# Softmax factors 1/sum: spread over partitions through HBM and multiplied on GpSimd, in place of products with the identity

## The chip, the cores and the metric

One core of a Trainium2 chip runs the whole program in one launch. The metric is the device time of one execution in microseconds (us); lower is better. Engines are named as in the profile: PE (TensorE, matmul), PEld (its weight loads), DVE (VectorE), ACT (ScalarE), POOL (GpSimd) and SP (SyncE, which here only issues DMAs). Each engine works through its own instructions in order.

## The reference, cut to what matters

The program is a stack of transformer-like layers on 512 tokens of width 1024 (and 256 context tokens): two layers with four branches each (two of them attention), then an even layer, an odd layer and feed-forward blocks. The change touches three places, all of the form softmax(scores) times values, where the division by the row sum of the exponentials is done at the end, on the product with the values:

```python
def _attend(q, k, v, sink):
    s = jnp.einsum('bqkgd,bnkd->bkgqn', q, k, ...)
    if sink is not None:
        ...
        p = jax.nn.softmax(jnp.concatenate([s, s_sink], axis=-1), axis=-1)[..., :-1]
    else:
        p = jax.nn.softmax(s, axis=-1)
    return jnp.einsum('bkgqn,bnkd->bqkgd', p.astype(v.dtype), v)
```

The places are the attention of layer 0 (tokens and context), that of layer 1 (tokens only), and the latent attention (MLA) of the odd layer, which runs beside a state-space group (S5) whose recurrence has 63 steps.

## The kernel before, in words

The program is written as generators over tiles; a scheduler then sets the order in which each engine gets its instructions, and pools of buffers with a fixed number of slots decide what an instruction has to wait for. Weights come from HBM over one queue of DMAs, which SP issues in order, through a few buffers that are used in turn.

Attention works on pairs of heads. For one pair, one block of 128 queries (`qi`) and one of its two heads (`j`) there is one item, and items pass through a pipeline of three steps: `scores` (PE matmuls, the row maximum on DVE, the exponential on ACT, which also gives the row sum), `transposes` (PE, with the copy out of PSUM by ACT or DVE into a tile named `pt`, or `hlo` in MLA) and `values` (PE, into one PSUM tile `po` in which head j stands on partitions 64 j to 64 j + 63, queries along the free axis). When the last query block of a pair is done, `normalised` is called with that `po` and the sums, which stand with queries on partitions. It takes the reciprocals (L1137), and PE brings each column of them onto 64 partitions by a product of the broadcast column with the identity (L1141, two per query block). ACT copies the result into SBUF (L1144), and DVE multiplies `po` with it (L1145).

There are 16 such calls: 8 in layer 0 (four of 4 query blocks, output `x`, four of 2, output `xc`), 4 in layer 1 (4 blocks, `y`) and 4 in MLA (4 blocks, output `hlo`). In MLA the result goes at once to a helper, `split`: ACT casts it to a high part `hhi` (L258), and POOL takes the rest `hlo` (L259). Both feed the output projection.

In MLA, `scores` also advances the S5 recurrence by a step or so (L2095 to L2099: five small DVE instructions a step, each step needing the one before it). After MLA, PE needs the finished states and some tables that SP fetches from HBM (`s5T`, `s5ca`).

Of the kernel before, what the change touches and what calls it, by code (L numbers as in the profile page):

```python
# [9 lines left out]
F32 = mybir.dt.float32  # L10
# [4 lines left out]
ALU = mybir.AluOpType  # L15
AX = mybir.AxisListType
PSUM = bass.MemoryType.PSUM
P = 128
# [78 lines left out]
class Kern:  # L97
# [254 lines left out]
    def silu_c(self):  # L352

        cc = self.vc[:, 0:16]
        t = self.tl(self.sm, [P, 16], F32, "siluc")
        self.S.activation(t, cc, AF.Tanh, scale=0.5)
        self.V.scalar_tensor_tensor(t, t, 1.0, cc, ALU.add, ALU.mult)
        self.sT = self.tl(self.cp, [P, 8, 32], F32, "sT")
        self.V.memset(self.sT, 0.0)
        for i in range(2):  # L360
            self.V.tensor_scalar(self.sT[:, :, i], t[:, 8 * i:8 * i + 8], 0.5, None, ALU.mult)
# [67 lines left out]
    def layer0_norm(self, i, hcp):  # L429

        xt, nt = self.toks[i]
        ss = self.tl(self.sm, [P, nt], F32, "l0ss")
        sq = self.tl(self.hp, [P, 1024], BF16, "hhi")
        for t in range(nt):
            self.S.activation(sq, xt[:, t, :], AF.Square, accum_out=ss[:, t:t + 1])
        r = self.rsq(ss, 1.0 / 1024, EPS, [P, nt], "nrm")
        for t in range(nt):
            self.V.tensor_scalar(xt[:, t, :], xt[:, t, :], r[:, t:t + 1], None, ALU.mult)
        n = nt * P
        xn = [self.tl(*((self.xp, [P, 512], F32, "x"), (hcp, [P, 256], F32, "xc"))[i]) for _ in range(8)]  # L440
        yield xn, n
        for k in range(8):
            ps = self.tl(self.tp, [P, 512], F32, "tp")
            for t in range(nt):
                self.T.transpose(ps[:, t * P:(t + 1) * P], xt[:, t, k * P:(k + 1) * P], self.ident)
            (self.S.copy if k % 2 else self.V.tensor_copy)(xn[k], ps[:, :n])
            if k == 3:
                yield
        yield
# [683 lines left out]

    def normalised(self, out, po, sums, nq, pool, tag, bufs=None):

        r = self.tl(self.sm, [P, 4, 2], F32, "rsm", bufs=2)
        self.V.reciprocal(r[:, :nq], sums[:, :nq])  # L1137
        pb = self.tl(self.tp, [P, 512], F32, "tp")
        for qi in range(nq):
            for j in range(2):  # L1140
                self.T.matmul(pb[64 * j:64 * j + 64, qi * P:(qi + 1) * P], r[:, qi, j:j + 1].to_broadcast([P, 64]),  # L1141
                              self.ident, start=True, stop=True)
        rb = self.tl(pool, [P, 512], F32, tag, bufs=bufs)
        self.S.copy(rb[:, :nq * P], pb[:, :nq * P])  # L1144
        self.V.tensor_tensor(out, po[:, :nq * P], rb[:, :nq * P], ALU.mult)  # L1145

    def run(self, gen):

# [689 lines left out]
class Kern3(Kern2):  # L1838
# [21 lines left out]

    def s5_alloc(self):
        dp = self.ctx.enter_context(self.tc.tile_pool(name="s5d", bufs=1, space=bass.MemoryType.DRAM))
        self.d_bm = [self.tl(dp, [P, 4, 2, P], F32, f"dbm{b}") for b in range(4)]
        self.d_ca = [self.tl(dp, [P, 2, 8, 64], F32, f"dca{b}") for b in range(4)]
        self.d_kk = self.tl(dp, [16, 32, 15 * 16], F32, "dkk")
        self.d_tt = [self.tl(dp, [P, 4, 4, P], F32, f"dtt{b}") for b in range(2)]
        self.a8 = self.tl(self.cp, [P, 2, 2, 16], F32, "a8")
# [500 lines left out]
```

## Time and profile before

| | |
|---|---|
| time, median of 3 runs | 2815.12 us (2809.93, 2815.12, 2815.5) |
| the profiled execution | 2810.49 us, of which the span is 2808.7 us |
| mean granted clock of TensorE | 0.991 |
| PE busy, share of the span | 2716.6 us, 97% |
| DVE busy | 1423.4 us, 51% |
| ACT busy | 1000.8 us, 36% |
| POOL busy | 895.9 us, 32% |

The span runs from the first to the last instruction; 1.8 us of the profiled execution lie outside it. Busy times are sums over the whole program, whose parts have different limits, and the ends of matmuls are modelled, so that a PE that shows as busy may still be waiting in part. What a change is worth in one part is read from that part.

### The profile page before, as it was taken

What the parts mean: (1) busy time and instruction counts of PE and PEld (TensorE: products, weight loads), DVE (VectorE), ACT (ScalarE), POOL (GpSimd) and SP (SyncE); (2) the same over time, 40 slices, a digit from 0 to 9 for tenths busy, and PEclk for the clock granted to TensorE, in tenths of its full rate; (3) what the DMA queues carried; (4) which work ended last, traced back from release to release, by engine and by line L of the source; (5) the groups of instructions that cost most, each with busy time, mean ns of one, the idle gap of its engine ahead of it and who ended that gap; (6) DMA issues with size and microseconds to landing.
All of it is one profiled execution on the core that took longest, in us unless ns stands there. A gap on an engine that the chain in (4) does not pass through costs nothing. (4 is left out here: it accounts for less than half of the span.)

```text
span 2808.7 us, 39749 instructions
## 1 busy us (share of the span) xinstructions
PE 2716.6 (97%) x15896; PEld 2269.8 (81%) x15896; DVE 1423.4 (51%) x2837; ACT 1000.8 (36%) x1802; POOL 895.9 (32%) x685
## 2 busy tenths in 40 slices
PE   6999999999998999999999989999999989999998
PEld 4976888888897888888998777788888876788888
DVE  5635511113255556435678787655542377655532
ACT  3335522222343553333445332322222244422322
POOL 4500343332234134333322232533333221333332
PEclk9999999999999999999999999999999999999999
DMA  7226122112222114342322231223223212332222
GB/s 247 68 87 201 61 64 75 58 59 66 93 75 90 46 50 121 119 133 75 95 84 75 50 98 35 71 91 105 91 98 97 80 54 83 99 104 90 96 96 87
DMA packets 221581, 250.33 MB, mean 89 GB/s; under 512 B 14351, under 2 KB 205428, under 8 KB 220116
## 3 DMA queue, kind: packets, MB, share of 16 engines
q1 hardware_dynamic: 219204, 242.86, 27.7%
q0 software_dynamic: 2192, 4.93, 0.9%
q8 instruction: 125, 2.05, 0.3%
q14 instruction: 60, 0.49, 0.1%
HBM read 233.64 MB, written 8.88 MB: 86 GB/s over the span
## 5 line engine op out<-in xcount | busy, mean ns | idle before, releaser
L234 POOL TENSOR_TENSOR wlo<-wraw,whi 128x1024 fp32r<-128x1024 f32 (+3 forms) x180 | 438.7, 2437 | 859.0 <-ACT whi L233 826.0
L233 ACT CAST whi<-wraw 128x1024 fp32r<-128x1024 f32 (+2 forms) x360 | 351.9, 1007 | 594.5 <-issue 201.0
L234 DVE TENSOR_TENSOR wlo<-wraw,whi 128x1024 fp32r<-128x1024 f32 (+2 forms) x180 | 235.9, 1310 | 376.9 <-ACT whi L233 376.4
L240 PE MATMUL ex<-hhi,wlo 128*128 128x512 f32 x1044 | 408.2, 391 | 7.1 <-DVE wlo L234 7.1
L238 PE MATMUL ex<-hhi,whi 128*128 128x512 f32 x1044 | 410.1, 393 | 0.6 <-ACT whi L233 0.6
L239 PE MATMUL ex<-hlo,whi 128*128 128x512 f32 x1044 | 408.0, 391 | 0.0
L238 PE MATMUL mm<-hhi,whi 128*128 128x512 f32 x708 | 281.7, 398 | 2.4 <-ACT whi L233 2.2
L239 PE MATMUL mm<-hlo,whi 128*128 128x512 f32 x708 | 278.7, 394 | 3.0 <-DVE hlo L330 2.6
L240 PE MATMUL mm<-hhi,wlo 128*128 128x512 f32 x708 | 278.9, 394 | 2.6 <-DVE wlo L234 2.5
L240 PEld LDWEIGHTS ex<-hhi,wlo 128*128 128x128 f32 x1044 | 196.6, 188 | 49.9 <-DVE wlo L234 8.6
L238 PEld LDWEIGHTS ex<-hhi,whi 128*128 128x128 f32 x1044 | 196.9, 189 | 41.9 <-ACT whi L233 1.6
L239 PEld LDWEIGHTS ex<-hlo,whi 128*128 128x128 f32 x1044 | 196.9, 189 | 39.5 <-issue 0.2
L238 PEld LDWEIGHTS mm<-hhi,whi 128*128 128x128 f32 x708 | 133.9, 189 | 32.5 <-issue 3.6
L240 PEld LDWEIGHTS mm<-hhi,wlo 128*128 128x128 f32 x708 | 133.6, 189 | 32.4 <-DVE wlo L234 3.8
L239 PEld LDWEIGHTS mm<-hlo,whi 128*128 128x128 f32 x708 | 133.9, 189 | 30.9 <-DVE hlo L330 3.9
L238 PE MATMUL mm<-whi,hhi 128*128 128x256 f32 (+1 forms) x464 | 135.2, 292 | 0.5 <-ACT hhi L258 0.5
L240 PE MATMUL mm<-whi,hlo 128*128 128x256 f32 (+1 forms) x464 | 133.2, 288 | 1.4 <-DVE hlo L330 1.4
L239 PE MATMUL mm<-wlo,hhi 128*128 128x256 f32 (+1 forms) x464 | 133.2, 287 | 0.9 <-DVE wlo L234 0.9
L238 PE MATMUL ex<-fhi,whi 128*128 128x512 f32 (+1 forms) x308 | 112.1, 364 | 0.0
L240 PE MATMUL ex<-fhi,wlo 128*128 128x512 f32 (+1 forms) x308 | 111.7, 363 | 0.0
L239 PE MATMUL ex<-flo,whi 128*128 128x512 f32 (+1 forms) x308 | 111.7, 363 | 0.0
L234 POOL TENSOR_TENSOR wblo<-wbraw,wbhi 128x256 fp32r<-128x256 f32 x32 | 27.0, 845 | 238.6 <-ACT wbhi L233 224.4
(823 smaller groups left out, 6019.6 us busy)
## 6 DMA issues: line engine op xcount, KB each, us to landing
wraw<-in_w_merge SPq DMA_DIRECT2D x32, 1024.0 KB
wraw<-in_ev_w_in SPq DMA_DIRECT2D x22, 1024.0 KB
wraw<-in_ffn_gate SPq DMA_DIRECT2D x22, 1024.0 KB
wraw<-in_ffn_up SPq DMA_DIRECT2D x22, 1024.0 KB
wraw<-in_w_in SPq DMA_DIRECT2D x20, 1024.0 KB
wraw<-in_ffn_down SPq DMA_DIRECT2D x17, 1024.0 KB
wraw<-in_w_ada SPq DMA_DIRECT2D x16, 1024.0 KB
wbraw<-in_w_br SPq DMA_DIRECT2D x32, 256.0 KB
```

Source lines behind the costliest of these rows:

```text
L233: self.S.copy(hi[:, a:b], raw[:, a:b])
L234: e.tensor_tensor(lo[:, a:b], raw[:, a:b], hi[:, a:b].bitcast(F32), ALU.subtract)
L238: self.T.matmul(ps, lh, rh, start=first, stop=False)
L239: self.T.matmul(ps, lh, rl, start=False, stop=False)
L240: self.T.matmul(ps, ll, rh, start=False, stop=last)
```

## The change

The reciprocals are written in the order of heads (8 columns, or 4). One PE transpose turns them into 8 rows of 128 (L1141 of the new file), DVE copies them to SBUF (`rrow`, one buffer), SP stores them to HBM (`drr`), and two further DMAs load them back, each spread over 64 partitions, into the tile `rb` that the product with the identity filled before. ACT copies `po` into `out`, and POOL multiplies `out` with `rb` in place. Two small tiles lose their second buffer.

```diff
     def normalised(self, out, po, sums, nq, pool, tag, bufs=None):
 
-        r = self.tl(self.sm, [P, 4, 2], F32, "rsm", bufs=2)
-        self.V.reciprocal(r[:, :nq], sums[:, :nq])
-        pb = self.tl(self.tp, [P, 512], F32, "tp")
-        for qi in range(nq):
-            for j in range(2):
-                self.T.matmul(pb[64 * j:64 * j + 64, qi * P:(qi + 1) * P], r[:, qi, j:j + 1].to_broadcast([P, 64]),
-                              self.ident, start=True, stop=True)
+
+        n = nq * P
+        r = self.tl(self.sm, [P, 8], F32, "rsm", bufs=1)
+        self.V.reciprocal(r[:, :2 * nq].rearrange("p (j q) -> p q j", j=2), sums[:, :nq])
+        pr = self.tl(self.tp, [P, 512], F32, "tp")
+        self.T.transpose(pr[:2 * nq, :P], r[:, :2 * nq], self.ident)
+        rows = self.tl(self.cp, [8, P], F32, "rrow")
+        self.V.tensor_copy(rows[:2 * nq], pr[:2 * nq, :P])
+        d = self.tl(self.drp, [8, P], F32, "drr")
+        self.nc.sync.dma_start(d[:2 * nq], rows[:2 * nq])
+        self.S.copy(out, po[:, :n])
         rb = self.tl(pool, [P, 512], F32, tag, bufs=bufs)
-        self.S.copy(rb[:, :nq * P], pb[:, :nq * P])
-        self.V.tensor_tensor(out, po[:, :nq * P], rb[:, :nq * P], ALU.mult)
+        for j in range(2):
+            self.nc.sync.dma_start(rb[64 * j:64 * j + 64, :n], d[j * nq:(j + 1) * nq].rearrange("q t -> (q t)").unsqueeze(0)
+                                   .to_broadcast([64, n]))
+        self.G.tensor_tensor(out, out, rb[:, :n], ALU.mult)
...
     def s5_alloc(self):
         dp = self.ctx.enter_context(self.tc.tile_pool(name="s5d", bufs=1, space=bass.MemoryType.DRAM))
+        self.drp = self.ctx.enter_context(self.tc.tile_pool(name="drr", bufs=4, space=bass.MemoryType.DRAM))
```

The scheduler lays the instructions out anew, and three places of the order matter below. Line numbers up to L1133 are the same in both files, and later ones are higher by 6 or 7 in the new one (the exponential of MLA is L2209 before and L2216 now, the row maximum L1297 and L1303).

ACT's order at the end of MLA's first pair, before: the copy of the spread factors (L1144), the cast of the normalised tile (L258), and behind it the exponentials of the next pair (L2209), each with what it waits for.

```order
L2209 ACTIVATE hhi_20628,sme_20569<-mat_20623,mx_20626 128x256 [waits DVE_49,Activation_49]
L1144 COPY hlo_20661<-tp_20652 128x512 [waits PE_49,Activation_49]
L258 CAST hhi_20647<-hlo_20649 128x512 [waits DVE_49]
L2209 ACTIVATE hhi_20671,sme_20569<-mat_20666,mx_20669 128x256 [waits DVE_49,Activation_49]
L2222 COPY hlo_20680<-tp_20678 128x128 [waits PE_49]
L2209 ACTIVATE hhi_20702,sme_20569<-mat_20697,mx_20700 128x384 [waits DVE_49,Activation_49]
```

The same place now: `hlo_20655` is the unscaled copy of `po`, and the cast of it waits for POOL, that is, for the multiplication.

```order
L2216 ACTIVATE hhi_20634,sme_20575<-mat_20629,mx_20632 128x256 [waits DVE_49,Activation_49]
L1146 COPY hlo_20655<-mpo_20509 128x512 [waits PE_49,Activation_49]
L2171 COPY mkT_20694<-tp_20696 64x512 [waits PE_49,Pool_49]
L258 CAST hhi_20653<-hlo_20655 128x512 [waits Pool_49]
L2216 ACTIVATE hhi_20676,sme_20575<-mat_20671,mx_20674 128x256 [waits DVE_49,Activation_49]
L2229 COPY hlo_20685<-tp_20683 128x128
L2216 ACTIVATE hhi_20707,sme_20575<-mat_20702,mx_20705 128x384 [waits DVE_49,Activation_49]
```

The cast keeps its place ahead of the next pair's exponentials, but what it waits for is now POOL instead of DVE. It is so at the end of the second and third pair too.

DVE's order at the end of MLA's last pair, before: from the copy of the last transposed block (L2222) over the last reciprocal to the first addition of the residual (L1283); between the reciprocal and the multiplication L1145 stand 25 instructions of the recurrence, and 17 behind that.

```order
L2222 COPY hlo_21166<-tp_21161 128x512
...
L1137 RECIPROCAL rsm_21192<-sme_20991 128x8
L2095 TENSOR_TENSOR s5ta_19926<-a_21_117,xp_3306_19848 128x32
...
L1145 TENSOR_TENSOR hlo_21191<-mpo_21106,hlo_21203 128x512
L2095 TENSOR_TENSOR s5ta_19926<-a_21_117,xp_3306_19848 128x32
...
L1283 TENSOR_TENSOR x_6687<-mm_21225,x_6687 128x512
```

The same place now, with the two copies of transposed blocks ahead of it.

```order
L2105 TENSOR_TENSOR xp_3330_19854<-s5ta_19932,s5tb_19933 128x32
L2106 TENSOR_TENSOR xp_3330_19854<-s5ta_19932,s5tb_19933 128x16
L2229 COPY hlo_21107<-tp_21104 128x256
L1303 TENSOR_REDUCE mx_21132<-mat_21129 128x1
L2229 COPY hlo_21145<-tp_21141 128x384
L1303 TENSOR_REDUCE mx_21154<-mat_21151 128x1
L2229 COPY hlo_21169<-tp_21164 128x512
L1139 RECIPROCAL rsm_21195<-sme_20995 128x4x2
L1143 COPY rrow_21199<-tp_21197 8x128
L1289 TENSOR_TENSOR x_6697<-mm_21227,x_6697 128x512
```

No step of the recurrence is left behind the last reciprocal: the 42 instructions that stood there (8.4 steps) have moved ahead. In the first interval between two reciprocals stand 17.0 steps now where 9.6 stood, in the second 14.4 (9.4), in the third 4.6 (8.4). In the first interval 10 steps stand together between two maxima, and only one copy (L2229) breaks them.

SP's order at the end of MLA, before: `s5T` and `s5ca` are the S5 tables (1 MB and 0.5 MB each).

```order
L226 DMA wraw_21517<-in_od_w_out 128x4x256 [waits DMAHW5_49,DVE_49,Pool_49]
L2256 DMA s5T_3603_21278<-dtt_19_115 128x2048 [waits PE_49,DVE_49,Activation_49,Pool_49]
L2261 DMA s5ca_3606_21282<-dca_14_110 128x1024
L2261 DMA s5ca_3607_21283<-dca_16_112 128x1024 [waits DMASW3_49,DMAHW2_49,DMASW2_49,DMASW0_49]
L2263 DMA s5T_3604_21279<-dtt_20_116 128x2048 [waits DMAHW3_49]
```

The same place now, from the last pair's store on.

```order
L1145 DMA drr_21201<-rrow_21199 8x128 [waits DMAHW5_49,DVE_49]
L2263 DMA s5T_3635_21280<-dtt_19_117 128x2048 [waits PE_49,DMAHW6_49,Activation_49,Pool_49]
L1149 DMA hlo_21204<-drr_21201 64x512 [waits DMAHW4_49,DMAHW5_49,DMAHW3_49,Pool_49]
L1149 DMA hlo_21204<-drr_21201 64x512 [waits DMAHW0_49]
L2268 DMA s5ca_3638_21284<-dca_14_112 128x1024 [waits DMAHW1_49]
L2268 DMA s5ca_3639_21285<-dca_16_114 128x1024 [waits DMASW3_49,DMASW2_49,DMASW0_49]
L2270 DMA s5T_3636_21281<-dtt_20_118 128x2048
```

The last pair's store stands first, the first S5 table between the store and the two loads of the factors, and the other tables behind them.

## Rows read from the trace of the kernel before

**Rows 1.** The page, part 1: busy time, share of the span, instructions.

```profile
PE 2716.6 (97%) x15896; PEld 2269.8 (81%) x15896; DVE 1423.4 (51%) x2837; ACT 1000.8 (36%) x1802; POOL 895.9 (32%) x685
```

**Rows 2.** Windows: length; busy us (instructions) of PE, PEld, DVE, ACT, POOL; clock, DMA.

```profile
206.00:275.00 69.00, 69.00 (x612) 45.74 (x610) 36.09 (x85) 37.52 (x89) 0.00 (x0) 1.00 0.61 196
275.00:315.00 40.00, 37.89 (x361) 30.42 (x360) 23.44 (x71) 27.12 (x69) 4.97 (x3) 1.00 0.33 105
940.00:1015.00 75.00, 74.41 (x683) 61.31 (x681) 40.59 (x84) 46.65 (x99) 10.83 (x7) 1.00 0.18 47
2297.00:2342.00 45.00, 44.84 (x353) 31.19 (x351) 43.32 (x199) 26.30 (x74) 6.51 (x7) 0.98 0.04 13
```

**Rows 3.** Line L1141: ns min/median/max, first and last start.

```profile
L1141 PE MATMUL tp<-cst,rsm x224: 272/273/323, 218.9 to 2351.8; 128*64 128x128 f32 x112
```

**Rows 4.** Timeline, two calls in layer 0 (start, us, engine, line).

```profile
218.87 1.04 PE L1141 MATMUL tp<-cst,rsm 128*64 128x128 f32 x16
219.85 0.39 PE L1076 MATMUL at<-tk,tq 128*128 128x256 f32 x1
...
228.62 0.66 PE L1141 MATMUL tp<-cst,rsm 128*64 128x128 f32 x8
```

**Rows 5.** Timeline, one PE transpose in MLA and what follows it.

```profile
2312.77 0.28 PE L2220 MATMUL tp<-cst,hhi 128*128 128x128 f32 x1
...
2312.89 0.81 PE L2203 MATMUL mat<-mkT,mqT 96*128 96x384 f32 x2
```

**Rows 6.** Waits of 206 to 320 us: total, times, longest.

```profile
PE at L1076 <- ACT e L1089: 1.7, 3, 0.7
```

**Rows 7.** Timeline, end of MLA's first pair.

```profile
2310.39 0.29 DVE L2222 COPY hlo<-tp 128x128 f32<-128x128 f32 x1
...
2311.11 1.14 PE L1141 MATMUL tp<-cst,rsm 128*64 128x128 f32 x15
...
2311.42 0.22 DVE L2095 TENSOR_TENSOR s5ta<-a,xp 128x32 f32<-128x32 f32 x1
...
2312.24 0.21 DVE L2095 TENSOR_TENSOR s5ta<-a,xp 128x32 f32<-128x32 f32 x1
...
2312.96 0.69 DVE L1145 TENSOR_TENSOR hlo<-mpo,hlo 128x512 f32<-128x512 f32 x1
...
2313.68 0.62 ACT L258 CAST hhi<-hlo 128x512 fp32r<-128x512 f32 x1 [0.76 <-DVE hlo L1145]
...
2314.32 0.47 ACT L2209 ACTIVATE hhi<-mat,mx 128x256 f32<-128x256 f32 x1
...
2314.45 1.27 POOL L259 TENSOR_TENSOR hlo<-hlo,hhi 128x512 fp32r<-128x512 f32 x1 [8.22 <-ACT hhi L258]
```

**Rows 8.** Timeline of SP's DMA issues (us of issuing), a store and load through HBM.

```profile
1238.53 4.82 SPq L1986 DMA_DIRECT2D dkk<-s5kk  x6
...
1245.35 2.07 SPq L1996 DMA_DIRECT2D dtt<-dkk  x3
```

**Rows 9.** DMA issues: count, KB each, median us to landing.

```profile
wf<-in_w_fnet POOLq DMA_DIRECT2D x2, 64.0 KB, 2.4
bsp<-in_b_sp POOLq DMA_DIRECT2D x4, 64.0 KB, 4.1
```

**Rows 10.** Timeline, end of MLA's last pair and start of S5.

```profile
2348.68 0.20 DVE L1137 RECIPROCAL rsm<-sme 128x8 f32<-128x8 f32 x1
...
2351.08 0.32 PE L1141 MATMUL tp<-cst,rsm 128*64 128x128 f32 x1
...
2354.38 1.30 DVE L2096 TENSOR_TENSOR s5tb<-a,xp 128x32 f32<-128x32 f32 x1
...
2355.67 0.50 PE L239 MATMUL mm<-hlo,whi 128*128 128x512 f32 x1 [0.39 <-POOL hlo L259]
...
2358.20 0.18 DVE L2099 TENSOR_TENSOR xp<-s5ta,s5tb 128x16 f32<-128x16 f32 x1
...
2360.79 0.67 PE L2273 MATMUL ex<-s5ca,xp 64*64 64x128 f32 x16
```

More of the change, by code (lines that the diff above doesn't have):

```diff
@@ L354, in silu_c @@
         cc = self.vc[:, 0:16]
-        t = self.tl(self.sm, [P, 16], F32, "siluc")
+        t = self.tl(self.sm, [P, 16], F32, "siluc", bufs=1)
         self.S.activation(t, cc, AF.Tanh, scale=0.5)
@@ L431, in layer0_norm @@
         xt, nt = self.toks[i]
-        ss = self.tl(self.sm, [P, nt], F32, "l0ss")
+        ss = self.tl(self.sm, [P, nt], F32, "l0ss", bufs=1)
         sq = self.tl(self.hp, [P, 1024], BF16, "hhi")
```

## The prediction, made before the changed kernel ran

> **What bounds the kernel now.** I began with the busy times of the page [rows 1]: PE is the only engine near its limit over the whole program, so an instruction taken from PE is worth something wherever PE really sets the pace. The windows by stage [rows 2] say where that is. In the attention of layer 0 (206 to 275 us) and layer 1 (940 to 1015) PE is busy for 69.00 of 69 and 74.41 of 75 us, and DVE and ACT are half idle. From 275 to 315 PE has 37.89 of 40, so a little is already waited for there. MLA (2297 to 2342) is another case: PE shows 44.84 of 45, but its ends are modelled, its weight loads fill only 31.19, and DVE is busy for 43.32 of 45, or 96%. DVE carries both the row maxima of the attention and the recurrence, and there I take it, with PE's chain, for the bound.
>
> **What is removed from PE.** The trace has 224 of the old products [rows 3]. They are pipelined, so their price is not 273 ns each: a group of 16 holds PE for 219.85 - 218.87 = 0.98 us [rows 4], a group of 8 for half, 0.49 (its busy time, 0.66, is the upper bound). One transpose takes their place. Transposes of 128x128 follow each other or another matmul after 0.12 us and show 0.28 busy [rows 5]; I take 0.12. Layer 0 saves 4 x 0.86 + 4 x 0.37 = 4.9 us, layer 1 saves 4 x 0.86 = 3.4, together **-8.3 us** where PE is the bound. With 0.28 it would be -6.4, and with 0.66 for a group of 8, -9.0. MLA's four calls are counted in its chain below.
>
> **What the new path costs in layers 0 and 1 (12 calls).** The result isn't wanted before the merge, much later, and ACT's copy of `po` waits only for PE. So the round trip through HBM is hidden by the items that follow, as long as there are buffers. Three things are not hidden for certain. `rb` holds one of the four `pt` slots until POOL has multiplied, some 7 us instead of 2; the order has copies into `pt` that now wait for POOL. POOL's multiplication can hold up DVE (next paragraph but one), and the maximum of an item with a sink is a DVE instruction of two SBUF operands ahead of an exponential. And the scheduler has put scores and exponentials in another order. Before, the waits of PE for exponentials were 1.7 us in three, 0.7 the longest [rows 6]. I take a wait of about half of 0.7 for each of the 12 calls, **+4 us**; the lower end is 0, the upper 12 x 0.7 = +8.
>
> **What it costs in MLA.** Here the cast of the normalised tile stands in ACT's order ahead of the exponentials of the next pair, and keeps that place (first piece of the order). Before, from the first of 15 products at 2311.11 to the next exponential at 2314.32 there were 3.2 us [rows 7]. Now the chain is: transpose 0.28 [rows 5]; copy to `rrow` 0.29, as the nearest DVE copy of 128 columns [rows 7]; issue of the store 0.7 and of the two loads 1.4 (issues on SP took 4.82/6 = 0.8 and 2.07/3 = 0.69 each [rows 8]); the store's landing; the loads' landing; the multiplication on POOL, 1.27 by the 512-column row, and the cast 0.62 [rows 7]. For the store, the last one to `dkk` was issued by 1243.35 and the load of it at 1245.35, so 2.0 us at most [rows 8]; for the loads, a 64 KB transfer showed 2.4 [rows 9]. Both are of another size or queue; the ends I keep are 1 and 4.1 us each (half the first row, and the slower 64 KB row of [rows 9]). With 2.0 and 2.4 the sum is 9.0 us, with the ends 6.6 and 12.8. ACT thus comes free for the next pair 5.8 us later than before, at three boundaries.
>
> [...]
>
> What hides this is the recurrence. A step takes 2312.24 - 2311.42 = 0.82 us of DVE [rows 7]. The order moves 8.4 steps from behind the last reciprocal to ahead of it, most of them into the first two boundaries, where DVE is then busy while ACT waits. But DVE was full already, so this only shifts the last reciprocal: +8.4 x 0.82 = +6.9, less 3 x (0.69 - 0.29) = 1.2 for the multiplications that leave DVE [rows 7]. In the third boundary only 1.6 steps and three maxima (about 2.6 us as an estimate, a maximum being put at half a step) are left between the copy to `rrow` and the copy that needs the exponentials. Of the chain 9.0 - 0.6 = 8.4 us come after `rrow`, so DVE and PE stand idle for about 5.8. At the end of the last pair there were 9.7 us from the products (2351.08) to the first use of `s5ca` (2360.79) [rows 10], PE filling them with the output projection. Now the chain to the cast takes 9.0, the issue of a 1 MB table stands between store and loads (0.7), POOL makes the low part after the cast (1.27), and a last matmul follows: about 11.5, so +1.8. Nothing of the recurrence hides that any more.
>
> One thing more speaks against the change. At 2354.38 a step's small DVE instruction took 1.30 us where one takes 0.21 [rows 7, 10]. It ran beside POOL's part of the last split, for which the matmul at 2355.67 then waits, so I read it as 1.1 us in which POOL held DVE. The four new multiplications are as long. In three of them DVE is in the recurrence; I take one hit in all, +1.0, the ends being 0 and 3.3.
>
> [...]
>
> MLA's sum is 6.9 - 1.2 + 5.8 + 1.8 + 1.0 = +14.3 us. Some will come back: the stretches without recurrence steps have a lighter DVE, and PE takes matmuls of the output projection into the boundaries, so that fewer are left at the end. I take **+12 us**, with ends of +4 (the short landings, and the idle time of the third boundary filled) and +21 (the long landings, three hits).
>
> **The sum** is -8.3 + 4 + 12 = about +7.7 us. Against the profiled execution (2808.7 of span and 1.8 around it, 2810.49) that is 2818. The profiled execution lies 4.6 us under the median of the runs, 2815.12, so I put the forecast at **2822 us**, +0.25%. Both ends together give -9.0 + 0 + 4 = -5 and -6.4 + 8 + 21 = +23, so 2810 and 2838.
>
> **Rivals.** (a) *Hidden in MLA, faster.* The total work of DVE in MLA falls (by 4 x 0.40 = 1.6 us), and if DVE alone sets the pace there, waits of ACT that DVE fills with steps of the recurrence cost nothing. The total would be -8.3 + 2 - 1.6 = about -8, 2807. For it speaks DVE's 96%; against it that the steps run out before the third boundary, and that nothing of DVE's work is left for the last chain. It decides if the chain after `rrow` is shorter than about 5 us, which wants landings near 1 us. (b) *Even.* MLA costs only 5 to 8 us, and the two sides cancel within 0.2% of the time (5.6 us, about what a measurement of this kernel can tell from no change). The rows for it are those of (a), with one boundary idle. (c) *The chain shows in the layers too.* If `rb` in a `pt` slot stops the transposes at each of the 12 calls for about 2 us (a chain of 9.0 against three items of the pipeline, some 7 us), 12 x 2 instead of 4 makes it +28, 2843. For it speak the new waits for POOL in the order, against it that ACT and DVE have half their time free there [rows 2].
>
> **How the numbers follow.** My forecast, slower by 6 to 23 us, has a chance of 0.52; (a) 0.15, (b) 0.24, (c) 0.09. So faster by over 0.2% 0.15, within it 0.24, slower 0.61. The range of 8 in 10 reaches from 2808 (most of (b), the upper part of (a)) to 2840.
>
> **What would show it.** Right: the L1141 group falls from 224 matmuls to 16 transposes; ACT's cast (L258) in MLA waits 4 us or more for POOL each time; PE has idle stretches of 3 us or more at the third boundary and at the end of MLA; the stretch of layer 1's attention becomes shorter by 2 us or more. Wrong: MLA's stretch from its first reciprocal to the first `s5ca` matmul doesn't grow by 4 us (then (a) holds), or the store and loads land in about 1 us each; or PE in layer 0 and 1 waits more than it saves (then (c)). The step I trust least is what the recurrence hides in MLA.

## The result, and the profile after

The changed kernel takes 2848.71 us (median of 4 runs, 2845.07 to 2851.14) against 2815.31 for the kernel before on the same chip (4 runs): a ratio of 1.0131, with a 95% interval of 1.0119 to 1.0143. It is slower by some 33 us where about 7 were forecast, and lies outside the 2810 to 2838 us of the forecast. Its profiled execution took 2847.89 us, with a span of 2846.0 and a mean granted clock of 0.985 (0.991 before).

Page of the changed kernel, part 1, which answers to [rows 1]:

```profile
PE 2727.9 (96%) x15688; PEld 2262.6 (79%) x15688; DVE 1426.5 (50%) x2837; ACT 999.0 (35%) x1802; POOL 915.5 (32%) x701
```

The 208 records taken from PE are gone (224 for 112 products before, 16 for 16 transposes now), and yet it shows 11 us more of busy time: what is left runs slower somewhere. Line L1141, with the store and POOL's multiplication in MLA (ns min/median/max, first and last start), answers to [rows 3]:

```profile
L1141 PE MATMUL tp<-cst,rsm x16: 271/273/273, 218.7 to 2378.7; 128*8 128x128 f32 x12, 128*4 128x128 f32 x4
L1145 SPq DMA_DIRECT2D drr<-rrow x16: 246/296/354, 219.3 to 2379.3; - x16
L1151 POOL TENSOR_TENSOR hlo<-hlo,hlo x4: 1261/1262/1311, 2324.7 to 2387.4; 128x512 f32<-128x512 f32 x4
```

Before, the first of the products began at 218.9 [rows 3] and the last call's first one at 2349.6 (shown below); now the two stand at 218.7 and 2378.7. So 29 of the 37.3 us by which the span grew are lost between them, and the other 8 behind. Windows of the changed kernel (columns as in [rows 2]):

```profile
206.00:275.00 69.00, 66.67 (x529) 41.46 (x527) 32.74 (x80) 33.99 (x82) 3.26 (x3) 1.00 0.64 205
2297.00:2342.00 45.00, 35.05 (x218) 23.07 (x219) 43.16 (x211) 20.71 (x59) 6.30 (x7) 0.85 0.10 31
2342.00:2395.00 53.00, 39.88 (x225) 24.66 (x225) 26.33 (x107) 15.32 (x42) 8.90 (x7) 0.84 0.21 75
```

In layer 0 PE now has 2.3 idle us of 69, where it had none. In MLA it is busy for 35.05 of 45 instead of 44.84, and the granted clock there is 0.85, where it was 0.98: PE waits, and in between it runs in part at half clock (a granted clock of 0.50 from 2326.7 to 2333.5). Not all of that drop is new: 6.8 us at half clock ahead of the first call (2299 to 2306) are a stretch that the kernel before has too, at 2292 to 2299, most of it outside the window.

To place the loss I matched the instructions of DVE, ACT and POOL that both kernels have (same line, same tile, same place in the count) and took the median shift of their starts in quiet stretches ahead of, between and behind the three attention stages. Differences of neighbouring shifts say by how much a stage grew: layer 0 +7.90 us, layer 1 -1.04, MLA with the following S5 products **+28.40**; the stretches between them +0.21 and +0.95. The same for every experiment, with its time:

| kernel | median us | ratio to before (95%) | layer 0 | layer 1 | MLA |
|---|---|---|---|---|---|
| changed | 2848.71 | 1.0131 (1.0119 to 1.0143) | +7.90 | -1.04 | +28.40 |
| e1_layers_new | 2819.46 | 1.0030 (1.0021 to 1.0039) | +8.08 | -1.09 | -0.64 |
| e2_mla_new | 2842.59 | 1.0106 (1.0089 to 1.0123) | +0.03 | -0.05 | +28.08 |
| e7_old_finish | 2847.75 | 1.0133 (1.0118 to 1.0148) | +8.20 | +0.17 | +27.52 |
| e6_old_spread | 2826.82 | 1.0064 (1.0046 to 1.0081) | +2.79 | +0.88 | +8.93 |
| e3_cast_pool | 2846.04 | 1.0124 (1.0109 to 1.0140) | +8.12 | -1.08 | +30.89 |
| e10_cast_pool_late_proj | 2848.62 | 1.0130 (1.0111 to 1.0150) | +7.96 | -1.08 | +31.03 |
| e9a_rec_first_new | 2849.22 | 1.0128 (1.0099 to 1.0158) | +9.61 | -1.02 | +29.13 |
| e9b_rec_first_old | 2815.51 | 1.0012 (1.0001 to 1.0022) | +0.01 | +0.01 | +1.77 |
| e11a_short_rec_new | 2844.94 | 1.0126 (1.0109 to 1.0143) | +7.96 | -1.07 | +23.19 |
| e11b_short_rec_old | 2811.36 | 1.0000 (0.9991 to 1.0009) | 0.00 | -0.10 | +0.36 |
| e13_three_freed | 2828.80 | 1.0061 (1.0048 to 1.0074) | +6.52 | -1.08 | +11.87 |
| e4_fill | 2852.73 | 1.0144 (1.0129 to 1.0159) | +9.76 | -1.05 | +30.72 |
| e4b_fill15 | 2841.29 | 1.0097 (1.0077 to 1.0118) | +7.63 | -1.07 | +18.35 |
| e17a_cast_only | 2852.52 | one run | +7.88 | -1.07 | +27.58 |
| e17b_cast_only_fill | 2837.13 | one run | +7.67 | -1.09 | +17.86 |
| e14a_slot_new | 2833.77 | 1.0082 (1.0067 to 1.0097) | -5.08 | -2.06 | +23.40 |
| e14b_slot_old | 2811.59 | 0.9997 (0.9988 to 1.0006) | -0.01 | +0.03 | +0.23 |
| e15_slot_layers_only | 2806.13 | 0.9984 (0.9975 to 0.9993) | -5.09 | -2.12 | -0.78 |

In the stretches between the stages, where the kernels have the same code, these shifts still change by up to 4 us, and between layer 1 and MLA by more than 6 in three profiles (e3, e10, e17a). In MLA the changed kernel, e2 and e14a have the same order on every engine and lost 28.4, 28.1 and 23.4. So a difference of 2 us in a layer, or of 5 in MLA, decides nothing by itself.

**MLA after.** The timeline from the end of the first pair, which answers to [rows 7] (start, us, engine, line; in brackets the idle time and what ended it):

```profile
2318.87 0.27 PE L1141 MATMUL tp<-cst,rsm 128*8 128x128 f32 x1
2319.18 0.28 DVE L1143 COPY rrow<-tp 8x128 f32<-8x128 f32 x1 [0.24 <-PE tp L1141]
2319.49 0.30 SPq L1145 DMA_DIRECT2D drr<-rrow  x1
2321.08 1.12 SPq L1149 DMA_DIRECT2D hlo<-drr  x2
...
2324.68 1.31 POOL L1151 TENSOR_TENSOR hlo<-hlo,hlo 128x512 f32<-128x512 f32 x1 [10.92 <-DMA hlo<-drr]
...
2324.89 1.16 DVE L2105 TENSOR_TENSOR xp<-s5ta,s5tb 128x32 f32<-128x32 f32 x1
...
2326.02 0.62 ACT L258 CAST hhi<-hlo 128x512 fp32r<-128x512 f32 x1 [3.54 <-POOL hlo L1151]
2326.69 0.80 PE L238 MATMUL mm<-hhi,whi 128*128 128x512 f32 x1 [3.72 <-ACT hhi L258]
...
2334.12 0.69 ACT L2216 ACTIVATE hhi<-mat,mx 128x512 f32<-128x512 f32 x1 [4.99 <-DVE mx L1303]
...
2340.88 0.27 PE L1141 MATMUL tp<-cst,rsm 128*8 128x128 f32 x1
...
2361.44 0.27 PE L1141 MATMUL tp<-cst,rsm 128*8 128x128 f32 x1
...
2378.67 0.27 PE L1141 MATMUL tp<-cst,rsm 128*8 128x128 f32 x1
```

The chain that was forecast is there, link by link: transpose 2318.87, copy 2319.18, store 2319.49, loads 2321.08, POOL 2324.68, cast from 2326.02 to 2326.64. That is 7.8 us, a little shorter than the forecast 9.0. What is not there is its price. From one call to the next lie 22.0, 20.6 and 17.2 us. Before, the first product of each of the four calls stood so:

```profile
2311.00 0.27 PE L1141 MATMUL tp<-cst,rsm 128*64 128x128 f32 x1
...
2325.28 1.04 PE L1141 MATMUL tp<-cst,rsm 128*64 128x128 f32 x16
...
2338.94 0.27 PE L1141 MATMUL tp<-cst,rsm 128*64 128x128 f32 x1
...
2349.64 0.32 PE L1141 MATMUL tp<-cst,rsm 128*64 128x128 f32 x1
```

That is 14.3, 13.7 and 10.7 us apart. So the three boundaries lost 7.7, 6.9 and 6.5 us, together 21.2. The rest, 7.6, is behind the last call: from there to the last matmul of `s5ca` it took 25.3 us and takes 32.8.

Three waits tell who stood in line. ACT waits 3.54 for POOL. PE waits 3.72 for ACT: a matmul of the output projection (L238), which needs that very tile, has been put into the boundary. And the first exponential of 512 columns waits 4.99 for a maximum of DVE and begins 7.5 us after the cast was done. The waits of 2316 to 2392 us (total, times, longest):

```profile
ACT hhi L258 <- POOL hlo L1151: 20.6, 4, 7.6
...
PE mm L238 <- ACT hhi L258: 12.6, 4, 4.0
```

And the windows of 6 us across the first boundary:

```profile
2318.00:2324.00 6.00, 4.96 (x37) 3.15 (x35) 5.58 (x29) 1.58 (x4) 0.00 (x0) 1.00 0.16 48
2324.00:2330.00 6.00, 3.31 (x7) 1.55 (x8) 5.69 (x25) 2.75 (x9) 2.58 (x2) 0.72 0.00 2
2330.00:2336.00 6.00, 5.30 (x28) 3.09 (x28) 5.72 (x28) 1.15 (x3) 1.23 (x2) 0.71 0.00 0
```

The reader is to see three things at once: DVE full, PE with 7 instructions in 6 us where [rows 7] has 15 in 1.14, and the clock at 0.72 and 0.71, mixed from stretches at 1.00 and 0.50. Each could be the reason.

### The profile page after: what moved, and what is told of

Its sections match the earlier page's. It is cut to its first block, busy times and chain, and to the rows that moved or that the text cites. A ratio compares the mean times of both kernels' runs of the same rounds, so it can differ in the third digit from the quotient of the medians.

```text
span 2846.0 us, 39499 instructions
## 1 busy us (share of the span) xinstructions
PE 2727.9 (96%) x15688; PEld 2262.6 (79%) x15688; DVE 1426.5 (50%) x2837; ACT 999.0 (35%) x1802; POOL 915.5 (32%) x701
## 4 chain that ended last, share of the span: by engine, by line
PE 43%; DVE 6%; DMA 2%; issue 1%; ACT 1%; POOL 1%; SPq 0%; ACTq 0%; POOLq 0%; DVEq 0%
PE ex L238 7%; PE ex L239 7%; PE ex L240 7%; PE mm L238 5%; PE mm L239 5%; PE mm L240 5%; DVE xs L1536 1%; PE sg L1700 1%; DVE wlo L234 0%; ACT whi L233 0%; PE mpo L2240 0%; DMA dcol<-in_ev_d_skip 0%; DMA dk<-dk 0%; PE mat L2210 0%; DMA hlo<-drr 0%
## 5 line engine op out<-in xcount | busy, mean ns | idle before, releaser
L234 POOL TENSOR_TENSOR wlo<-wraw,whi 128x1024 fp32r<-128x1024 f32 (+3 forms) x180 | 439.2, 2440 | 765.7 <-ACT whi L233 743.9
L234 DVE TENSOR_TENSOR wlo<-wraw,whi 128x1024 fp32r<-128x1024 f32 (+2 forms) x180 | 233.2, 1295 | 375.1 <-ACT whi L233 374.4
L238 PE MATMUL ex<-hhi,whi 128*128 128x512 f32 x1044 | 410.7, 393 | 0.6 <-ACT whi L233 0.5
L238 PE MATMUL mm<-hhi,whi 128*128 128x512 f32 x708 | 283.1, 400 | 15.0 <-ACT hhi L258 12.6
L238 PEld LDWEIGHTS ex<-hhi,whi 128*128 128x128 f32 x1044 | 196.8, 189 | 42.0 <-ACT whi L233 0.9
L238 PEld LDWEIGHTS mm<-hhi,whi 128*128 128x128 f32 x708 | 134.1, 190 | 45.7 <-ACT hhi L258 13.9
L238 PE MATMUL mm<-whi,hhi 128*128 128x256 f32 (+1 forms) x464 | 134.9, 291 | 2.6 <-ACT hhi L258 2.6
L238 PE MATMUL ex<-fhi,whi 128*128 128x512 f32 (+1 forms) x308 | 112.3, 365 | 0.0
L234 POOL TENSOR_TENSOR wblo<-wbraw,wbhi 128x256 fp32r<-128x256 f32 x32 | 26.8, 838 | 205.3 <-ACT wbhi L233 188.6
```

The lines of the kernel that those rows point to most:

```text
L234: e.tensor_tensor(lo[:, a:b], raw[:, a:b], hi[:, a:b].bitcast(F32), ALU.subtract)
L238: self.T.matmul(ps, lh, rh, start=first, stop=False)
```

## The experiments

### Which stage, and which half of the change

e1 gives MLA the old function and leaves the layers new; e2 the reverse.

```diff
-                self.normalised(on, po, st["s", m], 4, self.hp, "hlo")
+                self.normalised_p(on, po, st["s", m], 4, self.hp, "hlo")
```

> The new path in layers 0 and 1 (12 calls), the old products in MLA's four calls. By the shifts between the two traces (about +8 us gained over layer 0, -1 over layer 1, +29 over MLA), the theory that the three places add up expects +7 us against before, 2822, and MLA's stretch as before. A rival, that MLA's loss comes from something that the layers leave behind (loads that arrive later, a shifted queue), expects MLA's stretch long here too, and +20 us or more.

> The old products in layers 0 and 1, the new path in MLA alone. The theory that the places add up expects +29 us against before, 2844. The rival of e1 expects MLA's stretch near that of before, and less than +10 us.

Each stage keeps its own loss to within 0.7 us: +8.08 in layer 0 and -0.64 in MLA for e1, 0.03 and +28.08 for e2. So MLA isn't late because of anything the layers leave behind, and the two can be studied apart.

e7 spreads through HBM, but lets DVE multiply `po` as before; e6 keeps the products with the identity, and copies and multiplies in the new way.

```diff
# e7
-        self.S.copy(out, po[:, :n])
...
-        self.G.tensor_tensor(out, out, rb[:, :n], ALU.mult)
+        self.V.tensor_tensor(out, po[:, :n], rb[:, :n], ALU.mult)
# e6, behind the old products
+        self.S.copy(rb[:, :nq * P], pb[:, :nq * P])
+        self.S.copy(out, po[:, :nq * P])
+        self.G.tensor_tensor(out, out, rb[:, :nq * P], ALU.mult)
```

> The other half: the factors go through HBM, and DVE multiplies po with them as before, so that POOL has no part and DVE, in order, waits for the loads. If the round trip is what costs, layer 0 is slower by 6 us or more and MLA by 20 or more, at least as slow as the changed kernel. If the finish on POOL costs, layer 0 comes out at or under before.

> Half of the change: the factors are spread by the old products on PE, but the result is copied out by ACT and multiplied on POOL. No transfer through HBM. If the round trip is what costs, layer 0 gains or loses less than 2 us and MLA less than 8. If the finish on POOL costs (its hold on DVE, 1.27 more in the chain of MLA), layer 0 is slower by 4 or more and MLA by 10 or more.

The way through HBM alone costs as much as the whole change (+27.5 in MLA, +8.2 in layer 0). The new finish alone costs +8.9 in MLA and +2.8 in layer 0, which lies between the two expectations for e6 and decides for neither. The two halves add up to more than the whole (36.4 and 11.0 against 28.4 and 7.9). In MLA both hold up the same cast, which may be why; no run separates it.

### Is it ACT's queue, PE's, or DVE's?

e3 takes the cast from ACT, so that ACT can go on to the next pair's exponentials.

```diff
-                self.split(hi, lo, on, eng=G)
+                G.tensor_copy(hi, on)
+                G.tensor_tensor(lo, on, hi.bitcast(F32), ALU.subtract)
```

> The changed kernel, but the cast to the high part in MLA is done by POOL behind its multiplication, so that ACT's exponentials no longer stand behind the round trip. Theory A (ACT in order behind the cast is what stops the pairs) expects the three boundaries to fall back to their length of before within 2 us each, some 15 to 20 us of the 29 given back, 2828 to 2833 in all, with the loss at the end of MLA left. Theory B (DVE, full of recurrence steps that were moved, and held by GpSimd's multiplications, sets the pace) expects less than 8 us back, above 2840.

MLA stays at +30.9, so that nothing came back, as theory B had it. But PE also stands still in the boundary, for the tile and not for DVE; the timeline of e3:

```profile
2331.84 0.50 PE L238 MATMUL mm<-hhi,whi 128*128 128x512 f32 x1 [3.88 <-POOL hhi L2246]
...
2333.62 0.37 ACT L2229 COPY hlo<-tp 128x256 f32<-128x256 f32 x1 [4.41 <-PE tp L2227]
```

e10 adds that the projection's sums begin with the third pair's tile, so that none of its matmuls can be put into the first boundaries.

```diff
-        side = self.residual(yd, I["od_w_out_2"][0], 4)
+        side = self.residual(yd, I["od_w_out_2"][0], 4, ks=(2, 0, 1, 3))
```

> The changed kernel with the cast on POOL (as in the earlier run) and the output projection's sums begun with the third pair's tile, so that none of its matmuls can stand in the first two boundaries. Neither ACT nor PE then waits for the round trip there; DVE's order still has the bunched steps (17.4 and 12.6 in the first two intervals). Theory D expects the first interval between the transposes of two pairs, 22 us in the changed kernel, to fall to 17 or less, and the second from 20.5 to 17 or less. Theory B expects 20 to 22 and 18 to 20.

Again nothing: +31.0, with first intervals of 22.9 and 21.4 us, no shorter than theory B expected. The timeline of e10 shows the third queue:

```profile
2334.10 0.42 DVE L2234 COPY hlo<-tp 128x256 f32<-128x256 f32 x1
...
2334.57 0.90 PE L2232 MATMUL tp<-cst,hhi 128*128 128x128 f32 x3 [5.98 <-DVE hlo L2234]
...
2338.04 0.69 ACT L2221 ACTIVATE hhi<-mat,mx 128x512 f32<-128x512 f32 x1 [9.09 <-DVE mx L1308]
```

PE waits 5.98 us for a copy that stands on DVE behind a bunch of recurrence steps: what hid ACT's wait in the forecast is now the wait.

e9a and e9b try to take the bunch away by running the recurrence ahead (`advance(63)` at its definition), in the changed kernel and in the kernel before.

> The changed kernel with all 63 steps of the S5 recurrence emitted ahead of MLA's attention (the result is the same), so that DVE carries only the maxima and copies there. To be read against the next run, the kernel before with the same edit, in MLA's stretch from the first reciprocal to the last use of the S5 tables. Theory B (DVE full of moved steps sets the pace of the boundaries) expects the difference to fall from 29 us to 15 or less. If the round trip itself (ACT behind the cast, PE behind the projection) sets the pace, it stays at 22 or more.

> The kernel before with all 63 steps of the recurrence emitted ahead of MLA's attention: the control of the run before it. Both should lose the cover that the attention gave the recurrence, 63 x 0.82 = 52 us less what the projections hide, so 20 to 45 us slower than before.

This pair is inconclusive. Neither kernel became slower by the 20 us or more that were expected, because the scheduler moved only 5 steps: 32 instead of 27 stand ahead of the first reciprocal, so the bunches stayed (+29.1 and +1.8).

e11a and e11b cut the recurrence to 24 of its 63 steps, again in both kernels; 39 steps are left out of the computation.

```diff
-        V.memset(xp3[:, :, :, 0:1], 0.0)
+        V.memset(xp3, 0.0)
...
-            for c in range(63):
+            for c in range(24):
```

> The changed kernel with the S5 recurrence cut to its first 24 steps (39 steps are left out, their states stay zero, so the output isn't the reference's), all of which stand ahead of MLA's first reciprocal. From there on DVE has only maxima and copies. To be read against the next run, the kernel before with the same cut, from the first reciprocal to the last use of the S5 tables. Theory B (the moved steps on a full DVE set the pace) expects the 29 us between the two kernels to shrink to 12 or less. Theory E (the round trip itself leaves PE without work, whoever stands behind it, and the half clock stretches it) expects 20 or more to stay.

> The kernel before with the same cut (39 of 63 steps left out): the control. If DVE was what set the pace of MLA before, its stretch from the first reciprocal becomes shorter by 8 us or more; if PE did, by less than 4.

This is the plainest answer on the prediction's step about DVE. The kernel before doesn't gain from 39 steps less (ratio 1.0000, MLA +0.4): its calls stand within 1.4 us of where they stood, 14.4 and 14.1 us apart against 14.3 and 13.7, as the timeline of e11b shows.

```profile
2311.82 1.04 PE L1141 MATMUL tp<-cst,rsm 128*64 128x128 f32 x16
...
2326.22 1.04 PE L1141 MATMUL tp<-cst,rsm 128*64 128x128 f32 x16
...
2340.31 0.27 PE L1141 MATMUL tp<-cst,rsm 128*64 128x128 f32 x1
```

So the 96% that DVE shows there are no bound: the steps fill time that is left. And of the changed kernel's loss at most 28.4 - 23.2 = 5.2 us go with the steps, a difference that the clock alone can make (below). Theory E expected 20 or more to stay, and 23 did.

e13 joins e3, e10 and e11a: cast on POOL, projection late, 39 steps left out.

> The changed kernel with all three queues freed at MLA's boundaries: the cast on POOL, the output projection begun with the third pair's tile, and the recurrence cut to its first 24 steps (39 left out, so the output isn't the reference's). To be read against the kernel before with the same cut, whose transposes of the pairs stand 14.4 and 14.1 us apart. If the three in-order queues (ACT behind the cast, PE behind the projection, DVE behind the bunched steps) each hold the boundary alone, the first two intervals fall to 16 or less here, where freeing ACT alone, ACT and PE, or DVE alone left them at 19 to 23. If something else holds them (slots, the round trip itself), they stay at 18 or more.

The transposes of the four calls in e13's timeline:

```profile
2317.58 0.27 PE L1141 MATMUL tp<-cst,rsm 128*8 128x128 f32 x1
...
2331.30 0.27 PE L1141 MATMUL tp<-cst,rsm 128*8 128x128 f32 x1
...
2344.84 0.27 PE L1141 MATMUL tp<-cst,rsm 128*8 128x128 f32 x1
...
2361.50 0.27 PE L1141 MATMUL tp<-cst,rsm 128*8 128x128 f32 x1
```

Two intervals are 13.7 and 13.5 us, below the 14.4 and 14.1 of the control e11b. The round trip is as long as ever (5.9 and 5.5 us from transpose to POOL, 5.8 and 5.5 in the changed kernel) and costs nothing there, once none of the three queues has something of the next pair behind something that waits for it. Freeing one queue (e3, e11a) or two (e10) gave 5 us at most. In the third interval the projection is back in place, and PE alone holds the boundary:

```profile
2352.32 0.79 PE L238 MATMUL mm<-hhi,whi 128*128 128x512 f32 x1 [4.85 <-POOL hhi L2251]
```

The interval is 16.7 us, where the control has 10.7. With the end that leaves +11.9.

### The clock

e4b and e4 put 15 and 30 matmuls (the identity with itself, never read) into each of the three boundaries, ahead of the waiting ones, so that PE doesn't idle there.

```diff
+            if m > 8 and m % 8 == 2:
+                for _ in range(15):     # 30 in e4
+                    T.matmul(tp[:, 384:512], self.ident, self.ident, start=True, stop=True)
```

> The changed kernel, with 30 matmuls of the identity with itself (results unread, some 3.6 us of PE work) in the idle stretch of each of MLA's three boundaries, ahead of the next transposes. Theory C (PE falls to half clock after an idle stretch, and the matmuls after it take twice as long) expects a granted clock of 1.0 through the boundaries, and the time to fall by 5 to 12 us in spite of the added work, to 2837 to 2843. Without C (only the wait itself counts) the time stays or grows, 2848 to 2856.

> As the run with 30 filling matmuls, whose 30 took 6.8 us a boundary instead of the 3.6 meant (0.227 each): 15 now, 3.4 us. Its order, too, has no matmul of the output projection inside the boundaries. Theory C (half clock after idle time) together with theory D (the matmul of the output projection, pulled into the boundary, stops PE in order until the cast is there) expects MLA's loss to fall from 29 us to under 24. If DVE's order alone sets the pace (theory B), it stays at 27 to 31.

With 15, MLA's loss falls from 28.4 to 18.4 us, although work was added; with 30 it doesn't (30.7). Those took 6.8 us a boundary and not half of that, longer than the waits of 2.3 to 4.0 us that they were to fill: a product of the filling kind holds PE for 0.23 us. The windows of e4b across the first boundary, against those of the changed kernel above:

```profile
2318.00:2324.00 6.00, 5.98 (x43) 4.58 (x43) 5.77 (x28) 1.03 (x2) 0.53 (x1) 1.00 0.15 48
2324.00:2330.00 6.00, 4.14 (x25) 2.44 (x26) 5.72 (x24) 2.75 (x9) 2.65 (x3) 1.00 0.00 1
2330.00:2336.00 6.00, 5.59 (x47) 3.90 (x47) 5.90 (x28) 3.28 (x10) 0.68 (x1) 1.00 0.00 0
```

DVE is as full as before, but the clock stays at 1.00, and from 2330 to 2336 PE gets through 47 instructions instead of 28. This alone doesn't single out the clock, for the scheduler also changed the order: matmuls of the projection, steps, maxima and copies stand elsewhere in e4b.

e17a and e17b repeat this without the other two queues: e13 with the cast back on ACT (a), and the same with 15 filling matmuls (b). 39 steps of the recurrence are left out in both. Here DVE, ACT and POOL have the same order in both, and PE's differs by the filling and the place of three matmuls.

> The changed kernel with two of MLA's three queues freed (the output projection begun with the third pair's tile, the recurrence cut to 24 steps, 39 left out), and the cast left on ACT. If ACT behind the cast holds the boundary by itself, the first two intervals between the pairs' transposes stay at 17 to 20 us, against 13.7 and 13.5 with the cast on POOL. If not, 13 to 15.

> The run before it, with 15 matmuls of the identity with itself (unread, 3.4 us) in PE's idle stretch of each boundary; DVE and ACT have the same order. Theory C (the half clock after the idle stretch costs time of its own) expects the granted clock at 1.0 through the first two boundaries, and intervals shorter by 1.5 to 3 us each. Without it they are the same, or longer by the fill.

In e17a the intervals are 22.7, 19.6 and 17.6 us: the cast ahead of ACT's exponentials is enough by itself to hold the first two boundaries, and the loss is back (+27.6). Two windows of e17a behind the cast:

```profile
2330.00:2336.00 6.00, 2.58 (x4) 0.77 (x4) 0.00 (x0) 2.38 (x8) 2.92 (x3) 0.79 0.00 1
2336.00:2342.00 6.00, 6.00 (x26) 3.98 (x26) 2.11 (x4) 1.85 (x5) 0.81 (x2) 0.50 0.00 0
```

and those of e17b, whose call comes 6 us earlier:

```profile
2324.00:2330.00 6.00, 5.12 (x39) 3.78 (x39) 1.16 (x3) 2.75 (x9) 3.13 (x3) 1.00 0.01 2
2330.00:2336.00 6.00, 5.90 (x51) 4.27 (x49) 3.24 (x8) 3.48 (x11) 0.61 (x1) 1.00 0.00 0
```

After the wait PE is never idle in e17a, yet it does 26 instructions in 6 us, at 0.50, where e17b does 51 at 1.00. The first interval falls from 22.7 to 18.0 us, with 3.4 us of filling inside it, and MLA's loss from 27.6 to 17.9. So keeping PE at work is worth about 10 us of the 28. Each of the two ran once, and theory C came true only in part: e17b's second interval stayed at 20.5 (19.6 without filling), with a stretch at half clock of its own behind a wait.

A third comparison needs no filling. e14a (next section) changes the layers alone, and its MLA has the order of the changed kernel on every engine. Yet it lost 23.4 us there and not the 27 to 30 that were expected. The windows from the first call to the last `s5ca`, first of the changed kernel, then of e14a:

```profile
2319.00:2411.00 92.00, 72.46 (x501) 45.91 (x500) 49.97 (x213) 26.40 (x71) 14.14 (x12) 0.85 0.21 75
2304.00:2391.00 87.00, 68.16 (x501) 43.10 (x500) 49.63 (x213) 26.50 (x71) 14.20 (x12) 0.90 0.23 80
```

The same instructions take 5.0 us less, and the stretches at half clock in them come to 17.1 us instead of 27.3. So the same order, with much the same waits, doesn't always get the same clock.

### Layer 0

Two theories stood for +7.9: POOL's multiplications hold up DVE, or `rb` keeps one of the four slots of `pt` for the length of the round trip. e14a gives `rb` a slot of its own and `pt` one less, so that the memory is the same; e14b does the same to the kernel before.

```diff
-            pt = self.tl(ap, [P, 6, P], F32, "pt", bufs=4)
+            pt = self.tl(ap, [P, 6, P], F32, "pt", bufs=3)
...
-                self.normalised(Y(br, pair)[i][0], po, sums, nq, ap, "pt", 4)
+                self.normalised(Y(br, pair)[i][0], po, sums, nq, ap, "rbn", 1)
```

> The changed kernel, in whose layers 0 and 1 the spread factors have a buffer of their own, and the transposed blocks three instead of four slots. ACT's order there goes back to copies and exponentials in turn, as before. If the slot held for the round trip is what costs the 8 us in layer 0, layer 0 is faster here than in the control by 2 us or more; if the round trip costs in another way (SP's queue, DVE's copy, POOL), it is slower by 5 or more still. MLA +27 to +30 as in the changed kernel.

> The kernel before with the same buffers (own one for the factors, three for the transposed blocks): the control. The fourth slot was used by the factors once in four to two blocks, so I expect within 3 us of before.

Layer 0 goes from +7.90 to -5.08, layer 1 from -1.04 to -2.06, while the control stays at 0.0 in both. The slot it was. (In e6, without a round trip, the new finish still costs 2.8 in layer 0, with the shared slot.) What it does is seen in the order of ACT behind a call of 4 blocks (N the copy of `po` or of the factors, e an exponential, p a copy of a transposed block into `pt`):

```
before    N p e p e p e p e N
changed   N e e e p p p e p N
e14a      N p e p e p e p N
```

With a slot held, the copies into `pt` wait for POOL, and the scheduler sends three exponentials ahead of them. The timeline of the changed kernel has what follows:

```profile
279.78 0.73 POOL L1151 TENSOR_TENSOR xc<-xc,pt 128x256 f32<-128x256 f32 x1 [12.39 <-DMA pt<-drr]
...
280.69 0.58 ACT L1114 COPY pt<-tp 128x512 f32<-128x512 f32 x1
...
281.32 0.33 PE L1112 MATMUL tp<-cst,e 128*128 128x128 f32 x1 [2.27 <-ACT pt L1114]
```

POOL lets go of the slot at 280.51, ACT's copy begins at 280.69, and PE has waited 2.27 us for it. Here, too, the clock falls to 0.50 behind the wait, from 282.1 to 285.5. In the runs whose layer 0 has this same order the loss goes with such stretches: 6.5 us where there is none (e13), 7.6 to 8.1 with 3.4 us of it, 9.6 to 9.8 with 6.8 us (e9a, e4).

e15 keeps what won: the new way with its own slot in the layers, the old one in MLA.

> The new path in layers 0 and 1 with the buffer of its own, the old products in MLA: the version that the runs point to. If the slot theory holds, layer 0 gives back 2 to 5 us and layer 1 another 1 to 3, so 3 to 8 us under before, 0.997 to 0.999. If not, 1.002 to 1.004, as with the shared slot.

Layer 0 -5.1, layer 1 -2.1, MLA -0.8: 2806.13 us, ratio 0.9984 (0.9975 to 0.9993). It beats both kernels. Against the kernel before it is 0.16%, which is little, but the whole interval lies below 1.

## Why the prediction was wrong, step by step

**Products off PE, -8.3.** Right in layer 0, and hidden by the next point. With its own slot layer 0 measured -5.1 (forecast -4.9), layer 1 -2.1 (-3.4, of which some may have gone to waits). The 224 that the prediction calls products are records: the code issues 112 products, 8 for a call of 4 blocks, and each has two records. The price of a group, 0.98 us for such a call, doesn't depend on it.

**Waits in the layers, +4.** Mis-sized. The slot costs 7.90 + 5.08 = 13.0 us in layer 0, over 8 calls 1.6 each, and 1.0 in layer 1. Some 1.4 of the 13, as an estimate, are the half clock behind the waits (7.9 against the 6.5 of e13). The held slot is the mechanism of rival (c), which had put 2 us a call on it; it came near that in layer 0 and not in layer 1. The prediction named the held slot and then priced it by the longest old wait, 0.7 us [rows 6], a row that knew nothing of a slot held for a round trip (5.1 to 10.4 us from transpose to POOL in layer 0).

**The chain in MLA, 9.0.** Nearly right: 7.8 us at the first pair and 7.5 at the third. The store had landed within 1.3 us of the end of its issue at 2319.79, since the first load was issued at 2321.08; the loads landed 2.5 us after the end of theirs. So the two landings, 2.0 and 2.4 in the forecast, were 3.8 us at most.

**What hides it, +6.9 - 1.2 + 5.8 + 1.0.** This is the step that failed, and with it the first paragraph's "DVE ... I take it, with PE's chain, for the bound". I let the two first boundaries cost only the time of the steps moved ahead, since DVE "was full already". e11b shows that DVE's steps bound nothing before. The changed trace says it too: the last step of the recurrence came at 2364.7, 6.5 us later than before [rows 10], less than the 8.0 by which MLA began late, while the fourth call came 29.0 later. The steps took the place of idle time and the chain stayed on the path of the attention: items of the next pair stood behind a waiting instruction on ACT (e17a) and on PE (e13's third boundary), and behind the bunched steps on DVE (e10), each enough alone. That put 21.2 us on the three boundaries where about 12.5 were forecast.

**The end, +1.8.** Measured +7.6. First, the old end was read too short: the prediction counts 9.7 us from 2351.08 to the first use of `s5ca`, but 2351.08 is a later product of that call. From its first, at 2349.64, they are 11.15 us, and the forecast's own sum of 11.5 gives only some +0.4. Second, the loads come late, as the timeline of the changed kernel shows:

```profile
2378.67 0.27 PE L1141 MATMUL tp<-cst,rsm 128*8 128x128 f32 x1
...
2379.29 0.27 SPq L1145 DMA_DIRECT2D drr<-rrow  x1
...
2381.11 1.09 SPq L1149 DMA_DIRECT2D hlo<-drr  x2
...
2386.12 0.66 PE L2278 MATMUL ex<-s5T,U 128*64 128x128 f32 x8 [2.63 <-DMA s5T<-dtt]
...
2387.44 1.26 POOL L1151 TENSOR_TENSOR hlo<-hlo,hlo 128x512 f32<-128x512 f32 x1 [17.11 <-DMA hlo<-drr]
...
2389.40 1.22 PE L238 MATMUL mm<-hhi,whi 128*128 128x512 f32 x2 [2.63 <-ACT hhi L258]
```

From transpose to POOL it takes 8.77 us here and 5.81 at the first pair: 3.0 more, with the 1 MB table between store and loads, for which I had put 0.7 of issue. It isn't the issue: from the store to the loads it takes 1.82 us here and 1.59 at the first pair. From the end of the loads' issue to POOL it takes 5.24 instead of 2.48, so it is the loads that land later behind the table. Third, PE waits there not only for the cast (2.63) but also for the tables themselves, 2.63 us for `s5T` and 1.93 for the last `s5ca`, where the kernel before waits 0.39 at most. Around and behind these waits 10.2 us run at half clock. In e4b the end takes 29.0: its first two waits (2.58 and 2.23) and 6.8 us at half clock are there as well, the wait for `s5ca` and the stretch behind it aren't.

**Matmuls pulled into the boundaries.** I counted them as something given back, "so that fewer are left at the end". They gave nothing back: they wait for the tile that the round trip delays, 10.0 us in the three boundaries and 2.6 at the end, and hold up what stands behind them.

**The clock.** It isn't in the prediction at all. Between 2326 and 2395 the changed kernel has 23.9 us at half clock, behind PE's waits, and 3.4 more ahead of the last `s5ca`; the kernel before has none from its first call to the last `s5ca`. e17b wins back 9.7 us and e4b 10.0, by keeping PE at work (in e4b with a changed order), and e14a lost 5.0 less where the half clock was 10.2 us shorter. The granted clock is 0.50 behind a wait in e17a and 1.00 with the gap filled in e17b; how long a wait has to be to bring the clock down, no run shows.

**The POOL hit.** It occurred as said: beside POOL's multiplication at 2324.68 a step's small DVE instruction took 1.16 us where one takes 0.21. The maximum with a sink, which the prediction names for the layers, is hit as well: before, one took 1.20 us at 286.07, beside POOL's part of a weight split (L234), where it takes 0.16; in the changed layer 0 one took 0.39 at 306.90, beside the multiplication at 306.55. What the hit in MLA cost wasn't separated; with the steps left out of MLA (e11a) the loss is only 5.2 us smaller, so it is no more than that.

**What would show it.** The 16 transposes came as listed, and so did PE's idle stretch at the third boundary (3.98). ACT's waits for POOL were 3.54, 3.24, 6.17 and 7.63, the first two under the 4 that were named; PE's waits at the end were 2.63 and not 3; layer 1's gain of 2 us came only with the slot. And one sign of being wrong came true: in layer 0 PE waits more than it saves.

Open are the division between the queues of the 18 us that aren't the clock, since the queues replace each other, and how much of the end the tables cost: no run moves them. For the second boundary e2 and e14a give a hint: without any half clock in it the interval is 18.9 and 19.0 us, so of the 6.9 us lost there some 5.3 are the waits themselves.

## What to carry to other kernels

The round trip here, whose result isn't wanted until later, cost nothing only where on every engine nothing of the next item stood behind an instruction that waits for it (e13: intervals of 13.7 and 13.5 us against 14.4 and 14.1), and where it held no buffer of the pipeline (layer 0: -5.1 us, against +7.9 with the slot held): look at each in-order queue and each slot, because freeing one or two of the three here gave 5 of 28 us at most. An engine that shows 96% busy may be filling idle time, as DVE here (39 steps less, ratio 1.0000); cut its work in the old kernel before taking it for the bound. And count with a PE wait of a few microseconds what a half clock behind it may cost: here some 10 of 28 us (e17b against e17a).

## What the runs showed of the hardware

The clock's part was the surprise: with waits of PE of 1.6 to 4.0 us in an otherwise dense stage the changed kernel ran 27.3 us of it at half clock (0.50), and 3.4 us of useless matmuls in each boundary made it faster (ratio 1.0097 against 1.0131). Not every wait is followed by such a stretch. Between the second and the third call the changed kernel waits 2.26 us, then 1.56, and has 3.4 us at half clock; the interval is 20.6 us. With the same order, e2 waits 2.69 and 1.06 and e14a 2.38 and 1.45; they have no such stretch there, and the intervals are 18.9 and 19.0. And a store of 4 KB and its reload over 128 partitions took 5.2 us from the store's issue to POOL's start (2319.49 to 2324.68), and 8.2 behind a 1 MB load (2379.29 to 2387.44).
